# The first layer's attention of a two-layer encoder, issued in a written order

## The chip, the cores and the metric

The kernel runs on one core of one Trainium2 chip. The metric is the device time of one execution in microseconds (us), as the median of several runs. All arithmetic is on 32-bit floating point data. A profile of one execution shows every instruction of the engines: PE (TensorE, matmuls), DVE (VectorE), ACT (ScalarE), POOL (GpSimd), and SP (SyncE, which issues most transfers).

## The reference

An input of 256 tokens with 1024 features goes through two residual layers. Layer 0 has two mixers side by side on one input projection; layer 1 has another kind of attention; each layer ends with an MLP of 4096 hidden features with squared ReLU. The change concerns layer 0:

```python
hn = rms_norm(h, norm_mix_g[layer])
proj = hn @ ab_w_in[j]                                   # 1024 x 2304
qa, ka, va, qb, kb, vb = jnp.split(proj, split_ab, axis=-1)
# mixer A: 8 query heads, 2 key/value heads of 64, norm per head, rotary
qa = apply_rope(rms_norm(qa.reshape(b, s, 8, 64), a_q_norm_g[j]), cos_ax, sin_ax)
ka = apply_rope(rms_norm(ka.reshape(b, s, 2, 64), a_k_norm_g[j]), cos_ax, sin_ax)
o_a = gqa_attention(qa, ka, va)
# mixer B: 8 heads of 64, a bias by distance on the logits
o_b = dilated_attention(qb, kb, vb, rel_bias)
h = h + jnp.concatenate([o_a, o_b], axis=-1) @ ab_w_out[j]
```

## The kernel before, in words

**Weights.** All weights lie in HBM as chunks of 128 x 2048 numbers (1 MB), in the order of their use. SP loads a chunk into one of three `raw` buffers. `split_piece` splits it in pieces: ACT casts a piece to a rounded high part (`whi`, line 222), DVE subtracts to get the low part (`wlo`, line 223); each piece is 512 columns in the first five chunks and 1024 after them. There is room for the halves of four chunks. When the last piece of a chunk is split, SP is told to load the chunk three places on. A product is then three matmuls, high x high, high x low and low x high (`mm3`, lines 264 to 266). How far the splitting runs ahead is set by counters: each quarter chunk that PE uses calls `quarter`, which calls `pump`, which splits pieces up to `LEAD` = 4 quarters ahead.

**Layer 0.** Up to line 956 the order is written by hand: the projections of q, k and v of mixer A, their sums of squares, the rotation (`rope_a`), and the norms. `norms` runs on POOL: it adds the sums, raises them to the power -1/2 (line 325) and improves the result by one Newton step of four operations (lines 326 to 329), first for the 4 key norms, then for 18 numbers (16 query norms and the 2 of the row); three scalings follow. `scale_k` multiplies the rotated keys by their norms on DVE, `turn_k` transposes them on PE and copies them four times on ACT (`kdA`, each of two heads in its own half of the partitions and in the other half). Between these stand the steps of `qk_b(0)`, a generator: 4 + 4 steps of 12 matmuls for q and k of the first half of mixer B's heads, then the turn of q and the copies of k (`kdB` twice on ACT, `klB` on DVE).

**The attention** (`attention`) goes over 16 heads, 8 of A and 8 of B. A head has: scores on PE (line 850, 851), row maxima on DVE, exponentials with sums on ACT, a normalisation on DVE, four transposes on PE (line 407), a copy of these on ACT (`pts`), and for two heads together the products with the values on PE (line 396), copied as high part on ACT and low part on DVE to `OT`. Between the heads a filler feeds PE: the second half of mixer B's q and k, its values (`v_b`), and the first half of the output projection (`out_first`); `SHARE_AB` says how many of its steps go to each head. Here the program's order is only the input of a planner, which gives each engine an order of its own by costs and priorities, so that an engine may be ahead of the program's order. The second half of the output projection (`out_second`) and the MLP follow, also planned. PSUM has four banks for projections, two for scores, and two that transposes and value products share.

Of the kernel before, what the change touches and what calls it, by code (L numbers as in the profile page):

```python
# [111 lines left out]
SHARE_AB = (0, 2, 1, 0, 0, 1, 2, 2)  # L112
# [54 lines left out]
def encoder(ctx: ExitStack, tc: tile.TileContext, x, xg, wall, grow, const, onehot, relb, out):  # L167
# [34 lines left out]
    at = {"take": 0, "piece": 0, "quarter": 0}  # L202
# [9 lines left out]
    def split_piece(cast=nc.scalar.copy):  # L212

        i, q = divmod(at["piece"], 4)
        n = 2 if i >= 5 else 1
        at["piece"] += n
        if q % 2 == 0:
            parts[i, q // 2] = [wp.tile([P, CW // 2], F32R, name=z, tag=z, bufs=W_BUFS) for z in ("whi", "wlo")]
        hi, lo = parts[i, q // 2]
        raw = raws[i][:, 512 * q:512 * (q + n)]  # L220
# [16 lines left out]
    def quarter(n=2):  # L237

        at["quarter"] += 1
        pump(n)  # L240
# [68 lines left out]
    mhalf = cp.tile([P, 18], F32, name="mhalf")  # L309
# [45 lines left out]
    def attention(heads, fill, dst):  # L355
# [8 lines left out]
        def maxima(h):  # L364
            if h < n:
                prob[h] = sp.tile([P, NT, S], F32, name="prob", tag="prob", bufs=3)
                sums[h] = small(2)
                heads[h]["max"](h, sb[h], prob[h])
# [5 lines left out]
        def norm(h):  # L374
            if h < n:
                r = small(2)
# [50 lines left out]

    def scaled_softmax(scale, nscale):

        nb = {}  # L430

        def mx(h, sb, p):
            m, nb[h] = small(2), small(2)
# [47 lines left out]
    def out_first(name, src, acc):  # L481
        for c in range(2):
            i, w = take(name, c, 4)
# [163 lines left out]
    with tc.tile_pool(name="l0", bufs=1) as lp:  # L647
# [57 lines left out]
        sums = sp.tile([P, NT, 10], F32, name="sums", tag="sums", bufs=1)  # L705
        st = sp.tile([P, NT, 9], F32, name="st", tag="st", bufs=1)
        fa = lp.tile([P, NT, 9], F32, name="fa")
        kr = sp.tile([P, NT, P], F32, name="kr", tag="pts", bufs=3)
        part, rk = small(4), small(4)
        ua = cp.tile([P, NT], F32, name="ua")  # L710
        eu = small(2)
        qr = {}

        def rs0(t):
            return fa[:, t, 8:9]
# [10 lines left out]
        def sums_q(t):  # L726
            sq = work()
            nc.scalar.activation(sq, acc[t], AF.Square)
            nc.vector.reduce_sum(sums[:, t, 0:8], sq.rearrange("p (h e) -> p h e", e=64), axis=AX.X)

        def sums_k():
            sk = work()
            for t in range(NT):
                nc.scalar.activation(sk[:, cols(t)], acckv[t][:, :P], AF.Square)
            for t in range(NT):
                nc.vector.reduce_sum(sums[:, t, 8:10], sk[:, cols(t)].rearrange("p (h e) -> p h e", e=64), axis=AX.X)

        def norms():
            mean_of(part, ua)
            nc.gpsimd.tensor_scalar(eu, ua, EPS, None, op0=OP.mult)  # L740
            for t in range(NT):
                nc.gpsimd.tensor_scalar(sums[:, t], sums[:, t], 1.0 / 64, eu[:, t:t + 1], op0=OP.mult, op1=OP.add)
# [5 lines left out]
            f = fa.rearrange("p t h -> p h t")[:, 0:8]  # L748
            nc.gpsimd.tensor_scalar(fq, f, 0.125, None, op0=OP.mult)
            nc.gpsimd.tensor_scalar(nfq, f, -0.125, None, op0=OP.mult)  # L750
# [11 lines left out]
        def scale_k():  # L762
            for t in range(NT):
                for gq in range(2):
                    nc.vector.tensor_scalar(kr[:, t, cols(gq, 64)], kr[:, t, cols(gq, 64)],
                                            rk[:, 2 * t + gq:2 * t + gq + 1], None, op0=OP.mult)

        def turn_k():
# [14 lines left out]

        def spread():
            rsp = o_bank()
            row_scales(rsp, 0, rs0)
            nc.scalar.copy(rs_b, rsp[:, :S])

        def qk_b(half):
            i, w = take("qkB", 2 * half, 8)  # L790
# [10 lines left out]
            i, w = take("qkB", 2 * half + 1, 8)  # L801
            kb = mm_bank()
            for m in range(2):
                for z in range(2):
# [4 lines left out]
                    if (m, z) == (1, 1 - half):  # L809
                        for t in range(NT):  # L810
                            nc.scalar.activation(q[:, cols(t, S)], pb[:, cols(t, S)], AF.Copy, scale=rq0[:, t:t + 1])
                    quarter()
                    yield
            pt = mm_bank()
            for m in range(2):
                for t in range(NT):
                    nc.tensor.transpose(pt[:, m * S + t * P:m * S + t * P + P],
                                        q[:, t * S + m * P:t * S + m * P + P], flip)
            two = slice(2 * half, 2 * half + 2)
            stack(qB, halves(pt), (two, ALL))  # L820
            kf = work()
            nc.vector.tensor_tensor(halves(kf), halves(kb), rs_b[:, None, :].to_broadcast([P, 2, S]), op=OP.mult)
            for s in range(2):
                own, other = cols(s, 64), cols(1 - s, 64)
                hs = slice(4 * half + s, 4 * half + s + 3, 2)
                nc.scalar.copy(kdB[own, hs], halves(kf[own]))
                nc.vector.tensor_tensor(klB[own, hs], halves(kf[own]), kdB[own, hs].bitcast(F32), op=OP.subtract)
                nc.scalar.copy(kdB[other, hs], halves(kf[own]))
            yield

        def v_b():
            va = [mm_bank() for _ in range(NT)]
            for j in range(2):
                i, w = take("vB", j, 4)
# [25 lines left out]
        def head_b(h):  # L860
# [3 lines left out]
            def mx(n, sb, p):  # L864
                m, nb[0] = small(2), small(2)
# [4 lines left out]
                nc.vector.tensor_scalar(nb[0], m, -1.0, None, op0=OP.mult)  # L870
# [3 lines left out]
            def ex(n, sb, p, l):  # L874
                for i in range(NT):
                    nc.scalar.activation(p[:, i], p[:, i], AF.Exp, bias=nb[0][:, i:i + 1],
# [10 lines left out]
        with tc.manual_schedule():  # L887
# [62 lines left out]
            split(1)  # L950
            next(b0)
            turn_q(0)
            next(b0)
            split(1)
            for t in range(NT):
                rope_a(kr[:, t], acckv[t][:, :P], 2, 2, t)
            split(1)
            turn_q(1)
            next(b0)
            scale_k()  # L960
            for n in range(4):
                next(b0)
                if n < 2:
                    split(2)
            values_a()
            turn_k()
            next(b0)
            spread()
        for j in range(2):
            load_bias(j)  # L970

        oacc = {}
        def filler():
            b1 = qk_b(1)
            for _ in range(2):
                next(b1)
                yield
            yield from b0
            yield from b1
            yield from v_b()  # L980
            yield "second"
            yield from out_first("outA", OT, oacc)

        fl = filler()
        phase = [0]

        def fill(h, part):
            if phase[0] == 0:
                n = 1 if h < 7 else 100
            else:  # L990
                n = SHARE_AB[h - 8] if part == 0 and h < 16 else 0
            if h < 0:
                n = 1
            for _ in range(n):
                r = next(fl, None)
                if r == "second":
                    phase[0] = 1
                    return
                if r is None and n == 100:
                    return  # L1000

        attention([head_a(h) for h in range(HA)] + [head_b(h) for h in range(HB)], fill, OT)
        for _ in fl:
            pass
# [5 lines left out]
    with tc.tile_pool(name="l1", bufs=1) as lp:  # L1010
# [44 lines left out]
        def latent():  # L1055
# [6 lines left out]
            uu, eu, f = small(6), small(2), small(6)  # L1062
# [141 lines left out]
```

## Time and profile before

| what | value |
|---|---|
| median of 3 runs | 577.69 us (576.15 to 577.76) |
| the profiled execution | 576.51 us |
| its span, first to last instruction | 574.5 us |
| granted TensorE clock, mean over the span | 0.993 |
| PE busy, share of the span | 559.0 us, 97% |
| DVE busy | 397.8 us, 69% |
| ACT busy | 329.6 us, 57% |
| POOL busy | 39.6 us, 7% |

The span is what the profile's times count in; the execution takes 2.0 us more than its span. A line of the profile names the source line, the engine, the operation, what it writes and reads, and its shape. Ends of matmuls are modelled and overlap their followers, so that a busy PE is not yet a PE at its pace.

### The profile page before, as it was taken

The numbers are of one execution on the slowest core, as the hardware profiler recorded it, in microseconds if no ns is written. First come the engines' busy times: TensorE is split into PE (matmuls) and PEld (weight loads), VectorE is DVE, ScalarE is ACT, GpSimd is POOL, SyncE is SP. The second block draws the span as 40 slices with busy tenths as digits, with TensorE's granted clock in tenths as the row PEclk, the third lists the DMA queues.
The fourth block names the chain that finished last, engine by engine and source line by source line (L and its number), as shares of the span: only waits on it lengthen the run. The fifth ranks groups of instructions, "written<-read, shape, count | busy, mean of one in ns | idle before, by whom it ended". The sixth has DMA issues, their size and how long they took to land.

```text
span 574.5 us, 8124 instructions
## 1 busy us (share of the span) xinstructions
PE 559.0 (97%) x3044; PEld 463.0 (81%) x3044; DVE 397.8 (69%) x715; ACT 329.6 (57%) x609; POOL 39.6 (7%) x67
## 2 busy tenths in 40 slices
PE   8969999999999999999999999999999999999994
PEld 4869777788888888888889877678888888888884
DVE  4987998487666756666688888668566656756645
ACT  5858997465455454545556597756445454544513
POOL 3590000000000000000002100000000000000002
PEclk9998999999999999999999999999999999999998
DMA  8883263345455564555526223244545454554201
GB/s 282 352 283 139 74 227 127 143 163 204 174 193 184 184 219 152 214 176 191 185 108 221 74 97 124 74 163 167 201 165 211 166 209 163 204 203 164 74 1 73
DMA packets 16087, 96.64 MB, mean 168 GB/s; under 512 B 1794, under 2 KB 3074, under 8 KB 5296
## 3 DMA queue, kind: packets, MB, share of 16 engines
q1 hardware_dynamic: 15040, 94.38, 45.4%
q10 hardware_dynamic: 720, 1.07, 0.5%
q0 software_dynamic: 288, 0.68, 0.5%
q8 instruction: 24, 0.39, 0.3%
q14 instruction: 15, 0.12, 0.1%
HBM read 95.05 MB, written 1.06 MB: 167 GB/s over the span
## 4 chain that ended last, share of the span: by engine, by line
PE 83%; DVE 4%; ACT 3%; DMA 3%; POOL 3%; issue 2%; SPq 0%; POOLq 0%; DVEq 0%; ACTq 0%
PE s L537 19%; PE mm L265 14%; PE mm L264 14%; PE mm L266 14%; PE s L538 10%; PE o L396 3%; PE s L1161 2%; PE o L407 2%; DMA xh<-in_x 2%; DVE wlo L223 1%; DMA raw<-in_wall 1%; POOL sm L325 1%; PE o L457 1%; POOL sm L326 1%; ACT prob L439 1%
## 5 line engine op out<-in xcount | busy, mean ns | idle before, releaser
L223 DVE TENSOR_TENSOR wlo<-raw,whi 128x1024 fp32r<-128x1024 f32 (+1 forms) x182 | 208.7, 1164 | 99.4 <-ACT whi L222 99.0
L222 ACT CAST whi<-raw 128x1024 fp32r<-128x1024 f32 (+1 forms) x181 | 178.1, 1005 | 92.5 <-PE mm L266 46.4
L537 PE MATMUL s<-hTs,whi 128*128 128x512 f32 x480 | 168.6, 393 | 0.2
L538 PE MATMUL s<-hTs,wlo 128*128 128x256 f32 x480 | 134.5, 280 | 0.0
L537 PEld LDWEIGHTS s<-hTs,whi 128*128 128x128 f32 x480 | 90.1, 188 | 21.1 <-DVE hTs L465 1.1
L264 PE MATMUL mm<-whi,h2h 128*128 128x512 f32 x252 | 99.6, 396 | 0.0
L265 PE MATMUL mm<-wlo,h2h 128*128 128x512 f32 x252 | 99.5, 395 | 0.0
L266 PE MATMUL mm<-whi,h2l 128*128 128x512 f32 x252 | 99.0, 396 | 0.0
L538 PEld LDWEIGHTS s<-hTs,wlo 128*128 128x128 f32 x480 | 90.4, 188 | 1.4
L530 ACT CAST h2h<-work 128x256 fp32r<-128x256 f32 x64 | 25.5, 402 | 56.8 <-DVE work L529 56.8
L264 PEld LDWEIGHTS mm<-whi,h2h 128*128 128x128 f32 x252 | 47.3, 188 | 11.9 <-ACT h2h L530 0.9
L266 PEld LDWEIGHTS mm<-whi,h2l 128*128 128x128 f32 x252 | 47.2, 187 | 11.5 <-DVE h2l L531 0.3
L265 PEld LDWEIGHTS mm<-wlo,h2h 128*128 128x128 f32 x252 | 47.4, 188 | 9.8
L527 ACT COPY work<-s 128x256 f32<-128x256 f32 x60 | 22.1, 368 | 46.9 <-PE s L538 46.9
L528 DVE TENSOR_TENSOR work<-s,work 128x256 f32<-128x256 f32 x60 | 25.3, 422 | 17.3 <-ACT work L527 17.3
L531 DVE TENSOR_TENSOR h2l<-work,h2h 128x256 fp32r<-128x256 f32 x64 | 26.9, 423 | 14.6 <-ACT h2h L530 14.6
L529 DVE SCALAR_TENSOR_TENSOR work<-work 128x256 f32<-128x256 f32 x64 | 27.0, 425 | 2.1
L264 PE MATMUL mm<-whi,hTs 128*128 128x256 f32 (+1 forms) x80 | 27.8, 348 | 0.6 <-ACT hTs L904 0.6
L266 PE MATMUL mm<-whi,hTs 128*128 128x256 f32 (+1 forms) x80 | 27.2, 340 | 0.0
L265 PE MATMUL mm<-wlo,hTs 128*128 128x256 f32 (+1 forms) x80 | 27.1, 338 | 0.0
L265 PE MATMUL mm<-wlo,OT 128*128 128x512 f32 x64 | 26.3, 411 | 0.0
L264 PE MATMUL mm<-whi,OT 128*128 128x512 f32 x64 | 26.1, 408 | 0.0
(230 smaller groups left out, 775.2 us busy)
## 6 DMA issues: line engine op xcount, KB each, us to landing
raw<-in_wall SPq DMA_DIRECT2D x84, 1024.0 KB, 4.8
bias<-line_d SPq DMA_DIRECT2D x4, 384.0 KB, 4.2
raw<-in_wall SPq DMA_DIRECT2D x4, 256.0 KB, 5.6
raw<-in_wall SPq DMA_DIRECT2D x2, 512.0 KB, 7.4
xh<-in_x SPq DMA_DIRECT2D x1, 1024.0 KB, 11.6
xgt<-in_xg SPq DMA_DIRECT2D x2, 256.0 KB, 7.9
kc<-in_const SPq DMA_DIRECT2D x1, 512.0 KB, 8.8
grw<-in_grow POOLq DMA_DIRECT2D x1, 512.0 KB, 3.9
```

Of the source, the lines that this page charges most:

```text
L222: cast = cast(hi[:, s], raw)
L223: nc.vector.tensor_tensor(lo[:, s], raw, hi[:, s].bitcast(F32), op=OP.subtract)
L264: nc.tensor.matmul(out, ah, bh, start=first, stop=False)
L265: nc.tensor.matmul(out, ah, bl, start=False, stop=False)
L266: return nc.tensor.matmul(out, al, bh, start=False, stop=last)
L527: nc.scalar.copy(v[:, 0], bank[:, S:])
L528: nc.vector.tensor_tensor(v[:, 0], bank[:, :S], v[:, 0], op=OP.add)
L529: nc.vector.scalar_tensor_tensor(v[:, 1], v[:, 0], 0.0, v[:, 0], op0=OP.max, op1=OP.mult)
L530: nc.scalar.copy(hi, v[:, 1])
L531: nc.vector.tensor_tensor(lo, v[:, 1], hi.bitcast(F32), op=OP.subtract)
L537: nc.tensor.matmul(bank, wh, hTs[:, k].rearrange("p a t -> p (a t)"), start=k == 0, stop=False)
L538: nc.tensor.matmul(bank[:, S:], wl, hT[0][:, k], start=False, stop=k == 7)
```

## The change

Three things change in layer 0.

1. After the norms, nothing is planned any more: a string, `ORDER_AB`, says letter by letter which step comes next, and every engine takes its instructions in that order. The letters are: `c` cast of a piece on ACT, `l` its subtraction on DVE (with the load that it frees); `q`, `r` the turns of A's queries; `p`, `x`, `k` rotation, scaling and turn of A's keys; `n`, `m` norms and their scalings; `d`, `s` the spread of the row norm over partitions; `u` A's values; `i` the first bias loads; `a`, `b` the next step of `qk_b(0)` and `qk_b(1)`, `v` of B's values, `o` of the output projection's first half; and for the next head or pair `S` scores, `M` maxima, `E` exponentials, `N` normalisation, `T` transposes, `P` copy of these, `V` value products, `K` copies of their result. `pump` is off meanwhile.
2. POOL keeps the sums and the two powers. The Newton step becomes three operations on DVE (`newton`), for the keys and for the 18 others, the scalings of the norms and of the keys go to ACT.
3. Of A's keys, the copies in the other half read the first copies. Of B's keys, the copies in the other half are no longer made by ACT but by transfers from one half of the partitions to the other, issued from POOL's queue.

Small tiles of two numbers get 12 buffers instead of 4. The core of the diff:

```diff
-SHARE_AB = (0, 2, 1, 0, 0, 1, 2, 2)
+ORDER_AB = (
+    "clqcalclccrlclpcaacaxaanadlklaiSumaMsESbclbMESabSNTMablEcNNPbMSTcbPaTPElMlVb"
+    "KSNbEMcTPNvaETSlbcVMKNbPSvTENlcPMvbvlESTPMNvclbvVETSvNKMclbTPPScSMENvVETPMEN"
+    "SKvoMTPSNoVKcETSPMoElSNMNVTlcPKooTloEPMNETPNocVTPlKVKo")
...
-        cast = cast(hi[:, s], raw)
-        nc.vector.tensor_tensor(lo[:, s], raw, hi[:, s].bitcast(F32), op=OP.subtract)
-        if q + n == 4:
-            load(i + RAW_BUFS)
+    def split_piece(cast=nc.scalar.copy):
+        cast = cast_piece(cast)
+        low_piece()
         return cast
...
         at["quarter"] += 1
-        pump(n)
+        if not at["hand"]:
+            pump(n)
...
         def norms():
-            rsqrt(sums[:, :, 8:10], 4, rk)
-            nc.gpsimd.tensor_copy(st[:, :, 0:8], sums[:, :, 0:8])
-            nc.gpsimd.tensor_copy(st[:, :, 8], ua)
-            rsqrt(st, 18, fa.rearrange("p t h -> p (t h)"))
-            nc.gpsimd.tensor_scalar(rq0, fa[:, :, 8], 0.125, None, op0=OP.mult)
-            nc.gpsimd.tensor_scalar(fq, f, 0.125, None, op0=OP.mult)
-            nc.gpsimd.tensor_scalar(nfq, f, -0.125, None, op0=OP.mult)
+            for n in (slice(0, 2), slice(2, 11)):
+                nc.gpsimd.tensor_tensor(fa[:, :, n], sums[:, :, n], mhalf...[:, :, n], op=OP.pow)
+        def newton(n):
+            u, y = sums[:, :, n], fa[:, :, n]
+            nc.vector.scalar_tensor_tensor(u, u, -0.5, y, op0=OP.mult, op1=OP.mult)
+            nc.vector.tensor_tensor(u, u, y, op=OP.mult)
+            nc.vector.scalar_tensor_tensor(y, u, 1.5, y, op0=OP.add, op1=OP.mult)
+        def norms_end():
+            newton(slice(2, 11))
+        def scales():
+            nc.scalar.activation(rq0, fa[:, :, 10], AF.Copy, scale=0.125)
+            nc.scalar.activation(fq, f, AF.Copy, scale=0.125)
+            nc.scalar.activation(nfq, f, AF.Copy, scale=-0.125)
         def scale_k():
+            newton(slice(0, 2))
             for t in range(NT):
                 for gq in range(2):
-                    nc.vector.tensor_scalar(kr[...], kr[...], rk[...], None, op0=OP.mult)
+                    nc.scalar.activation(kr[...], kr[...], AF.Copy, scale=fa[:, t, gq:gq + 1])
...
                 nc.scalar.copy(kdA[own, s], pk[own, :S])
-                nc.scalar.copy(kdA[other, s], pk[own, :S])
+            for s in range(2):
+                nc.scalar.copy(kdA[other, s], kdA[own, s].bitcast(F32))
...
                 nc.scalar.copy(kdB[own, hs], halves(kf[own]))
+            yield
+            for own, other, hs in sides:
                 nc.vector.tensor_tensor(klB[own, hs], halves(kf[own]), kdB[own, hs].bitcast(F32), op=OP.subtract)
-                nc.scalar.copy(kdB[other, hs], halves(kf[own]))
+                nc.gpsimd.dma_start(kdB[other, hs], kdB[own, hs])
...
-        attention([head_a(h) for h in range(HA)] + [head_b(h) for h in range(HB)], fill, OT)
+            steps = {"a": b0, "b": qk_b(1), "v": v_b(), "o": out_first("outA", OT, oacc),
+                     **attention_steps([head_a(h) for h in range(HA)] + [head_b(h) for h in range(HB)], OT)}
+            for c in "".join(ORDER_AB).replace(" ", ""):
+                next(steps[c]) if c in steps else once[c]()
+        at["hand"] = False
```

`attention_steps` holds the same instructions as `attention`, each step of a head as a function of its own. In `qk_b` the scaling of q, the turn of q, the split of q, the copies of k and their low parts with the transfers are now steps of their own at the end.

## Rows read from the trace of the kernel before

**Rows 1.** Busy time by stretch: PE, PEld, DVE, ACT, POOL; granted clock; DMA.

```profile
38.60:43.30 4.70, 0.03 (x1) 0.00 (x0) 2.39 (x3) 1.24 (x4) 3.82 (x7) 1.00 0.74 258
43.30:47.10 3.80, 3.77 (x19) 3.77 (x20) 1.33 (x4) 3.46 (x6) 0.00 (x0) 0.55 0.57 233
47.10:106.00 58.90, 58.58 (x379) 46.62 (x379) 49.99 (x137) 49.89 (x118) 0.00 (x0) 1.00 0.39 139
106.00:118.60 12.60, 12.60 (x61) 9.99 (x60) 8.74 (x11) 6.58 (x13) 0.00 (x0) 1.00 0.38 129
118.60:125.00 6.40, 6.28 (x38) 5.18 (x36) 6.05 (x8) 4.47 (x8) 1.08 (x2) 1.00 0.31 100
125.00:300.00 175.00, 175.00 (x879) 146.66 (x880) 113.84 (x164) 86.44 (x132) 0.00 (x0) 1.00 0.51 186
```

**Rows 2.** Timeline of PE: first and last of the stage, the gap, the slow stretch.

```profile
27.40 0.60 PE L759 MATMUL o<-kc,qr 128*128 128x128 f32 x4
...
43.33 0.39 PE L850 MATMUL s<-kdA,qA 128*128 128x256 f32 x1 [4.71 <-ACT kdA L775]
...
43.85 0.42 PE L266 MATMUL mm<-whi,hTs 128*128 128x256 f32 x1
...
47.06 0.32 PE L265 MATMUL mm<-wlo,hTs 128*128 128x256 f32 x1
...
118.40 0.39 PE L266 MATMUL mm<-whi,OT 128*128 128x512 f32 x1
```

**Rows 3.** Timeline of POOL, where the norms are, and later in layer 1.

```profile
30.77 0.66 POOL L326 TENSOR_TENSOR sm<-sm 128x4 f32<-128x4 f32 x1
...
33.01 3.23 POOL L325 TENSOR_TENSOR sm<-st,mhalf 128x18 f32<-128x18 f32 x1
36.32 4.75 POOL L326 TENSOR_TENSOR sm<-sm 128x18 f32<-128x18 f32 x1
...
317.13 0.21 POOL L326 TENSOR_TENSOR sm<-sm 128x6 f32<-128x6 f32 x1
```

**Rows 4.** Timeline of DVE, beside the norms.

```profile
33.59 0.69 DVE L223 TENSOR_TENSOR wlo<-raw,whi 128x512 fp32r<-128x512 f32 x1
...
36.37 4.63 DVE L223 TENSOR_TENSOR wlo<-raw,whi 128x1024 fp32r<-128x1024 f32 x4
```

**Rows 5.** Timeline of PE: distances from start to start, kind by kind.

```profile
35.06 0.28 PE L264 MATMUL mm<-hTs,whi 128*128 128x256 f32 x1
...
36.00 0.28 PE L266 MATMUL mm<-hTs,wlo 128*128 128x256 f32 x1
...
60.38 1.08 PE L396 MATMUL o<-pts,vA 128*64 128x256 f32 x8
...
63.10 0.60 PE L407 MATMUL o<-kc,prob 128*128 128x128 f32 x4
63.45 0.37 PE L265 MATMUL mm<-hTs,whi 128*128 128x256 f32 x1
...
112.33 0.40 PE L265 MATMUL mm<-wlo,OT 128*128 128x512 f32 x1
...
113.73 0.39 PE L265 MATMUL mm<-wlo,OT 128*128 128x512 f32 x1
```

**Rows 6.** Timeline of ACT: one copy of mixer A keys.

```profile
42.55 0.35 ACT L774 CAST kdA<-o 64x256 fp32r<-64x256 f32 x1
```

**Rows 7.** The casts of the weights (line L222) from 20 to 106 us.

```profile
L222 ACT CAST whi<-raw x27: 604/1048/1096, 20.3 to 101.3; 128x1024 fp32r<-128x1024 f32 x19, 128x512 fp32r<-128x512 f32 x8
```

**Rows 8.** Groups of ACT instructions from 47 to 107 us: busy us, mean ns.

```profile
L410 ACT COPY pts<-o 128x512 f32<-128x512 f32 x16 | 9.4, 585 | 0.7 <-PE o L407 0.4
...
L876 ACT ACTIVATE prob<-prob,sm 128x256 f32<-128x256 f32 x16 | 8.0, 504 | 0.7 <-DVE sm L377 0.7
```

**Rows 9.** DMA issues from POOL's queue: KB, us to landing.

```profile
grw<-in_grow POOLq DMA_DIRECT2D x1, 512.0 KB, 3.9
oh<-in_onehot POOLq DMA_DIRECT2D x1, 66.0 KB, 6.6
```

More of the change, by code (lines that the diff above doesn't have):

```diff
@@ L201, in encoder @@
     raws, parts, done = {}, {}, set()
-    at = {"take": 0, "piece": 0, "quarter": 0}
+    at = {"take": 0, "piece": 0, "quarter": 0, "low": [], "hand": True}
     def load(i, pieces=1):
@@ L210, in load, with cast_piece @@
             nc.sync.dma_start(raws[i][:, s], wall[i, :, s])
-    def split_piece(cast=nc.scalar.copy):
+    def cast_piece(cast=nc.scalar.copy):
         i, q = divmod(at["piece"], 4)
@@ L426, in attention, with attention_steps, scores, maxima @@
         values(n // 2 - 1)
+    def attention_steps(heads, dst):
+        n = len(heads)
+        sb, prob, sums, pts, banks, out = {}, {}, {}, {}, {}, {}
+        def scores(h):
+            sb[h] = s_bank()
+            heads[h]["scores"](sb[h])
+        def maxima(h):
+            prob[h] = sp.tile([P, NT, S], F32, name="prob", tag="prob", bufs=3)
+            sums[h] = small(2, 12)
+            heads[h]["max"](h, sb[h], prob[h])
+        def exps(h):
+            heads[h]["exp"](h, sb.pop(h), prob[h], sums[h])
+        def norm(h):
+            r = small(2, 12)
+            nc.vector.reciprocal(r, sums[h])
+            for i in range(NT):
+                nc.vector.tensor_scalar(prob[h][:, i], prob[h][:, i], r[:, i:i + 1], None, op0=OP.mult)
+        def turned(h):
+            flipped = heads[h]["flip"]
+            banks[h] = t_bank()
+            for c in range(NT):
+                for i in range(NT):
+                    q = NT - 1 - i if flipped else i
+                    nc.tensor.transpose(banks[h][:, c * S + q * P:c * S + q * P + P], prob[h][:, i, cols(c)],
+                                        flip if flipped else ident)
+        def kept(h):
+            pts[h] = sp.tile([P, 512], F32, name="pts", tag="pts", bufs=3)
+            nc.scalar.copy(pts[h], banks.pop(h))
+        def values(j):
+            out[j] = o_bank()
+            for c in range(NT):
+                for s in range(2):
+                    nc.tensor.matmul(out[j][64 * s:64 * s + 64, :S], heads[2 * j + s]["v"](c),
+                                     pts[2 * j + s][:, cols(c, S)], start=c == 0, stop=c == NT - 1)
+        def split_values(j):
+            ob = out.pop(j)
+            nc.scalar.copy(dst[0][:, j], ob[:, :S])
+            nc.vector.tensor_tensor(dst[1][:, j], ob[:, :S], dst[0][:, j].bitcast(F32), op=OP.subtract)
+        return {c: map(f, range(k)) for c, f, k in (
+            ("S", scores, n), ("M", maxima, n), ("E", exps, n), ("N", norm, n), ("T", turned, n), ("P", kept, n),
+            ("V", values, n // 2), ("K", split_values, n // 2))}
     def scaled_softmax(scale, nscale):
@@ L482, in out_first @@
         for c in range(2):
-            i, w = take(name, c, 4)
+            i, w = take(name, c, 4, not at["hand"])
             acc[c] = [mm_bank() for _ in range(NT)]
@@ L774, in turn_k @@
                 nc.scalar.copy(kdA[own, s], pk[own, :S])
-                nc.scalar.copy(kdA[other, s], pk[own, :S])
+            for s in range(2):
+                own, other = cols(s, 64), cols(1 - s, 64)
+                nc.scalar.copy(kdA[other, s], kdA[own, s].bitcast(F32))
             for s in range(2):
@@ L782, in values_a, with spread_d @@
                 nc.scalar.activation(vA[:, t], acckv[t][:, P:2 * P], AF.Copy, scale=rs0(t))
+        dgs = []
+        def spread_d():
+            for t in range(NT):
+                dgs.append(sp.tile([P, P], F32, name="dg", tag="dg", bufs=4))
+                nc.vector.tensor_scalar(dgs[t], ident, rs0(t), None, op0=OP.mult)
         def spread():
             rsp = o_bank()
-            row_scales(rsp, 0, rs0)
+            for t in range(NT):
+                nc.tensor.matmul(rsp[:, cols(t)], ones, dgs[t], start=True, stop=True)
             nc.scalar.copy(rs_b, rsp[:, :S])
         def qk_b(half):
-            i, w = take("qkB", 2 * half, 8)
+            i, w = take("qkB", 2 * half, 8, False)
             pb = mm_bank()
@@ L800, in qk_b @@
                     yield
-            i, w = take("qkB", 2 * half + 1, 8)
+            i, w = take("qkB", 2 * half + 1, 8, False)
             kb = mm_bank()
@@ L808, in qk_b @@
                         done.add(i)
-                    if (m, z) == (1, 1 - half):
-                        for t in range(NT):
-                            nc.scalar.activation(q[:, cols(t, S)], pb[:, cols(t, S)], AF.Copy, scale=rq0[:, t:t + 1])
                     quarter()
                     yield
+            for t in range(NT):
+                nc.scalar.activation(q[:, cols(t, S)], pb[:, cols(t, S)], AF.Copy, scale=rq0[:, t:t + 1])
+            yield
+            kf = work()
+            nc.vector.tensor_tensor(halves(kf), halves(kb), rs_b[:, None, :].to_broadcast([P, 2, S]), op=OP.mult)
             pt = mm_bank()
@@ L818, in qk_b @@
                                         q[:, t * S + m * P:t * S + m * P + P], flip)
+            yield
             two = slice(2 * half, 2 * half + 2)
             stack(qB, halves(pt), (two, ALL))
[L821 to L825, printed above, removed]
+            yield
+            sides = [(cols(s, 64), cols(1 - s, 64), slice(4 * half + s, 4 * half + s + 3, 2)) for s in range(2)]
+            for own, other, hs in sides:
                 nc.scalar.copy(kdB[own, hs], halves(kf[own]))
+            yield
+            for own, other, hs in sides:
                 nc.vector.tensor_tensor(klB[own, hs], halves(kf[own]), kdB[own, hs].bitcast(F32), op=OP.subtract)
-                nc.scalar.copy(kdB[other, hs], halves(kf[own]))
+                nc.gpsimd.dma_start(kdB[other, hs], kdB[own, hs])
             yield
@@ L949, in encoder @@
             norms()
[L950 to L1000, printed above, removed]
@@ L1002, in encoder @@
[L1002 to L1004 removed]
+            oacc = {}
+            steps = {"a": b0, "b": qk_b(1), "v": v_b(), "o": out_first("outA", OT, oacc),
+                     **attention_steps([head_a(h) for h in range(HA)] + [head_b(h) for h in range(HB)], OT)}
+            once = {"c": cast_piece, "l": low_piece, "d": spread_d, "s": spread, "n": norms_end, "m": scales,
+                    "q": lambda: turn_q(0), "r": lambda: turn_q(1), "k": turn_k, "u": values_a, "x": scale_k,
+                    "p": lambda: [rope_a(kr[:, t], acckv[t][:, :P], 2, 2, t) for t in range(NT)],
+                    "i": lambda: [load_bias(j) for j in range(2)]}
@@ L1006, in encoder @@
+            for c in "".join(ORDER_AB).replace(" ", ""):
+                next(steps[c]) if c in steps else once[c]()
+            assert all(next(z, "end") == "end" for z in steps.values()) and not at["low"]
+        at["hand"] = False
     out_second("outA", OT, oacc, G_MLP)
```

55 lines of the change are left out of this document (30 added, 25 removed).

## The prediction, made before the change was run

> **What bounds the kernel now.** I read the busy time by stretch first. PE is busy in almost all of the span, and after the first layer's attention it does not stop (175.00 of 175.00 us between 125 and 300) [rows 1], so whatever the attention gives up shifts the rest to the left one for one. Inside the stage there is one hole, 38.6 to 43.3, in which PE does nothing, and behind it a stretch at a granted clock of 0.55 [rows 1]. The timeline of PE names the releaser: the first score matmul waits 4.71 us for the copied keys [rows 2], and the keys wait for the norms. The timeline of POOL shows why these are late: the 18-wide power takes 3.23 us, and then a multiply of 18 numbers takes 4.75, where one of 6 takes 0.21 elsewhere [rows 3]. DVE runs four subtractions of weights back to back in those very microseconds [rows 4]: POOL stands until DVE lets go. Elsewhere in the stage PE shows as busy, so its loss has to be found by distances from start to start.
>
> I count PE's work from 27.40 (the first turn of q) to the end of the first output projection, 118.40 + 0.23 = 118.63 [rows 2], by the loops of the code and the distances of [rows 5]: 192 matmuls of 256 columns for q and k of mixer B and 64 for scores at 0.94/8 = 0.1175 are 30.1 us; 144 of 512 columns (values of B, output projection) at 1.40/6 = 0.2333 are 33.6; 24 groups of four transposes or spreads at 0.35, plus 0.09 for the change of kind (0.37 busy for 0.28), are 10.6; the turn of k 0.25; 8 value products at 1.05 (the 1.08 overlaps its follower) are 8.4. Sum 82.9. The stretch is 91.23 long, so PE lost 8.3 us: 4.7 in the hole, 1.45 at the low clock (15 matmuls in 47.06 - 43.85 = 3.21 us instead of 1.76), and 2.2 in small waits of a few tenths.
>
> **The change part by part.**
>
> *Norms.* Four Newton operations, two copies and three scalings leave POOL; the two powers stay. The first power ends at 30.7, and the 18-wide one can start at 30.77, where the first multiply stood, instead of 33.01, and ends at 30.77 + 3.23 = 34.0 [rows 3]. DVE takes six small operations (0.1 to 0.2 us each, 0.7 in all; DVE has no row for them in this form, so I bound them by 0.3 and 1.5; the upper end is worth 0.8). By the written order DVE stands before them with the same pieces that it finished at 36.37 [rows 4], so the norms are ready at about 36.7, not 42.0, and the power has 2.7 us to spare. A hold of POOL by the two 512-wide subtractions that DVE has there (0.69 each [rows 4]) costs nothing.
>
> *First score.* After the norms: four scalings of k, now on ACT and narrower than the copy of [rows 6], some 0.26 each; the turn of k, 0.4; four copies of keys at 0.35 [rows 6], of which two now read the first two; handoffs of 0.05 to 0.1. With the norms of k at 36.4 that is 36.4 + 1.1 + 0.7 (PE is in a step of B) + 0.4 + 1.4 = 40.0 to 40.1. PE has until 27.40 + 12.4 = 39.8 the 96 matmuls of the first half of B (11.3 us) and three turns (1.1), written ahead of the first score. So the hole shrinks from 4.7 to 0.3 us, and the low clock behind it goes.
>
> *Order.* I then walked the string: every engine takes its instructions as written, each starts when the engine is free, its inputs have landed and its buffer is released. From the first score to the ninth (first head of B) PE meets no wait, so S8 starts at 40.1 + 26.7 = 66.8 (8 scores 3.8, spread 0.4, 8 steps of b 11.3, 6 turns of probabilities 2.6, 2 value products 2.1, 2 turns of B 0.9, 4 steps of v 5.6). Behind that I find new waits, all on ACT or the buffers. (1) At the first step of o, 78.9: its second bank of four in rotation is that of v, which ACT empties only after P8, a cast, E9, E10, P9, E11 and K3, that is 0.5 + 1.0 + 1.0 + 1.0, a wait for T9, then 0.5 + 1.0 + 0.3 and 0.7 for the copy, durations by [rows 7, 8] (an E is two of 0.50, copies scale with their width): PE waits 1.6. (2) At the last value product: turns and value products rotate through two banks, and its bank is that of V6, free once P15, then K6's copy and K6's subtraction are done; T15 covers 0.4, PE waits 1.6. In the kernel before the output projection's second half fills such places; a written region ends before it. (3) T9, V5 and the rest: 0.7. With the 0.3 these are 4.2 us. So the region ends at 27.40 + 70.4 + 4.2 = 102.0 and the output projection (48 x 0.2333, three turns: 12.5) at 114.5 instead of 118.63: 4.1 us gained. Whether PE's clock falls for a wait of 1.6 us no row shows; after the 4.71 it did. The bounds are 0 and 1.45 for each of the two; I take 0, for the clock is 1.00 in every other stretch of [rows 1].
>
> *Second key copies.* ACT loses four copies of B's keys at 0.6 (2.5 us) and POOL issues four transfers. The first half's keys are copied at 53.2 and needed at 66.8; the second half's at 70.7, issued by 71.4, and needed at S12, 78.5. Rows of POOL's queue land in 3.9 and 6.6 us [rows 9]: 75.3 to 78.0, so nothing is lost, with 0.5 us to spare at the slower one.
>
> *Weights.* The string holds 20 casts, 5 narrow and 15 wide. The kernel before had done 19 wide ones at the same point of PE's work (106.1) [rows 7], because its order lets ACT run ahead. Four wide pieces, 4 x 1.16 = 4.6 us of DVE (4.63 for four [rows 4]), move behind the region, where DVE is busy 8.74 of 12.60 and 6.05 of 6.40 [rows 1]. Only two of the seven pieces in that stage are needed before 114.5 and five before 123, and DVE idles 3.9 us there, so most is hidden. Between 0 and 4.6 I take 0.5, near the lower end since the free time is there.
>
> Sum: 8.3 - 4.2 - 0.5 = 3.6 us gained. The profiled execution took 576.51, and would take 572.9; the median of the runs is 577.69, 1.18 above it, and I predict for the median 574.1. About 0.3%, 1.7 us, is what a measurement can tell from no change.
>
> **The rivals.** *New waits don't appear* (o's bank is free earlier, the last value product finds its bank): 3.2 more, 577.69 - 6.8 = 570.9. For it speaks that these two waits each hang on a row of handoffs that may be shorter; against it, that the buffers are as few as before. Chance 0.13.
>
> *Hand-offs cost more than I took.* A fixed order has no planner's slack: at five places PE waits behind some six hand-offs each; 0.1 us more at each is 5 x 0.6 = 3.0: 577.1. The 2.2 us of small waits before speak for it. Chance 0.16.
>
> *The norms still come late.* If POOL's power held DVE as DVE held POOL's multiply, DVE's subtractions would stand for 3.2 us, Newton would end at 39.9 and the first score at 43.3: 574.1 + 3.2 = 577.3, or 578.8 if the low clock returns. The rows speak against it: DVE's subtraction at 33.59 took 0.69 in the middle of POOL's power [rows 3, 4]. Chance 0.06. The Trainium skill (SBUF — State Buffer, SBUF: two separate sides) calls the shared pair of ports an exclusive lock that whoever starts first keeps for a whole instruction. By that rule the time would be 577.3, by the rows 574.1; the trace agrees for POOL behind DVE (4.75 for 0.21), and differs for DVE behind POOL (0.69 as ever).
>
> *Slower: the transfers are held.* POOL must write their descriptors, and POOL can be held: if both transfers of the second half were held like the multiply, 2 x 4.75 + 6.6 = 16.1 from 70.7 is 86.8, S12 would be 8.3 late; 1.3 of it hides in o's wait: +7.0, 581.1. It decides from a landing of about 12.5 us on. Against it: DVE's longest run there is one wide subtraction (1.2 us) and a few short ones, not four. Chance 0.05. The same section of the Trainium skill warns that a transfer issued from POOL starves for descriptors while DVE has the pair; no row here shows such a transfer.
>
> *Split debt.* If the four pieces stand ahead of the turns for the MLP in DVE's queue, PE waits up to 4.6 there: 574.1 + 4.1 = 578.2. Against it speaks DVE's 3.9 us of free time. Chance 0.06.
>
> **How the numbers follow.** The forecast holds 0.54, with its own range 572.3 to 575.9. Faster by over 0.3% (below 576.0) are the forecast, the first rival and a little of the second: 0.54 + 0.13 + 0.03 = 0.70. Within 0.3%: 0.12 of the second, 0.05 of the late norms, 0.04 of the debt: 0.21. Slower (above 579.4): the held transfers 0.05 and the worse ends of the other three 0.04: 0.09. Leaving out some 0.05 below and 0.15 above, and holding the two bounds of the clock (574.1 + 2.9 = 577.0), the range is 570.9 to 577.5.
>
> **What would show it.** The first score starts near 40 and PE's gap before it is under 1 us, with a clock of 1.00 from 38 to 48. POOL has no multiply, and its wide power ends near 34 to 35. PE waits for ACT's copy of v at the first step of o, and for a bank at the last value product, some 1.6 us each; the output projection ends near 114.5. POOL's transfers land within 7 us. The prediction is wrong if PE waits more than 5 us in all between 40 and 102, if a weight-load wait appears between 114 and 125, or if the clock falls again.

## The result and the profile after

The kernel after takes 568.03 us (567.76 to 568.15), the kernel before, run beside it, 577.13: a ratio of 0.984, with a 95% interval of 0.983 to 0.986. The change gains 9.1 us; 3.6 were forecast, and the time lies 2.9 us below the low end of the range. The span fell from 574.5 to 566.0.

Busy time by stretch of the kernel after (PE, PEld, DVE, ACT, POOL; granted clock; DMA), to be read beside [rows 1]:

```profile
25.70:38.90 13.20, 12.97 (x108) 12.57 (x107) 12.39 (x33) 10.66 (x24) 6.82 (x7) 1.00 0.48 180
38.90:47.10 8.20, 8.20 (x71) 8.18 (x70) 7.56 (x15) 7.63 (x25) 0.00 (x0) 1.00 0.59 216
47.10:98.00 50.90, 50.90 (x325) 40.62 (x323) 44.11 (x123) 42.21 (x100) 2.49 (x4) 1.00 0.45 152
98.00:110.70 12.70, 12.70 (x65) 10.03 (x65) 12.23 (x16) 9.18 (x16) 0.00 (x0) 1.00 0.67 248
125.00:300.00 175.00, 175.00 (x911) 148.53 (x910) 115.84 (x163) 88.26 (x133) 3.06 (x4) 1.00 0.51 183
```

The hole and the stretch at a clock of 0.55 are gone. The timeline of PE in the kernel after, beside [rows 2]:

```profile
20.37 1.02 PE L1019 MATMUL o<-oh,rb 33*8 33x512 f32 x2
...
25.74 0.60 PE L833 MATMUL o<-kc,qr 128*128 128x128 f32 x4
...
36.84 0.33 PE L846 MATMUL o<-kc,kr 128*128 128x128 f32 x1
37.32 0.33 PE L846 MATMUL o<-kc,kr 128*128 128x128 f32 x1
...
38.92 0.28 PE L938 MATMUL s<-kdA,qA 128*128 128x256 f32 x1
...
79.01 0.39 PE L276 MATMUL mm<-whi,OT 128*128 128x512 f32 x1
...
96.09 0.66 PE L469 MATMUL o<-kc,prob 128*128 128x128 f32 x4
96.50 0.47 PE L277 MATMUL mm<-wlo,OT 128*128 128x512 f32 x1
...
97.73 0.40 PE L276 MATMUL mm<-whi,OT 128*128 128x512 f32 x1
98.06 1.08 PE L480 MATMUL o<-pts,vB 128*64 128x256 f32 x8
...
110.74 0.39 PE L601 MATMUL s<-hTs,whi 128*128 128x512 f32 x1
```

The first score starts at 38.92 and not at 43.33. The second bank of the output projection's first step is written at 79.01 without a wait, and between the last transposes (96.09) and the last value product (98.06) stand six matmuls of the output projection. The MLP begins at 110.74 and not at 118.63: 7.9 of the 8.5 us of span are gained by then. One row of ACT's timeline in the kernel after belongs to this, the copies of mixer B's values out of their banks:

```profile
79.82 1.27 ACT L931 ACTIVATE vB<-mm,fa 128x512 f32<-128x512 f32 x2
```

The norms in the kernel after, on POOL and then on DVE, beside [rows 3, 4]:

```profile
28.89 4.62 POOL L807 TENSOR_TENSOR fa<-sums,mhalf 128x4 f32<-128x4 f32 x2
...
69.65 1.23 POOL L916 DMA_DIRECT2D kdB<-kdB  x2 [16.43 <-ACT kdB L912]
```

```profile
29.72 1.33 DVE L230 TENSOR_TENSOR wlo<-raw,whi 128x512 fp32r<-128x512 f32 x2
...
36.50 0.18 DVE L815 SCALAR_TENSOR_TENSOR fa<-sums,fa 128x18 f32<-128x18 f32 x1
```

The two powers end at 33.5, and DVE's two subtractions under them took 0.67 each; one beside an idle POOL, at 24.60, took 0.69. The transfers of mixer B's second key copies landed after 4.0 us (median of 4); the last two were issued by 70.9, and the first score that reads them starts at 77.75 without a wait.

### The profile page after: what moved, and what is told of

Its sections match the earlier page's. It is cut to its first block, busy times and chain, and to the rows that moved or that the text cites. A ratio compares the mean times of both kernels' runs of the same rounds, so it can differ in the third digit from the quotient of the medians.

```text
span 566.0 us, 8115 instructions
## 1 busy us (share of the span) xinstructions
PE 555.5 (98%) x3044; PEld 461.6 (82%) x3044; DVE 399.1 (71%) x717; ACT 328.5 (58%) x612; POOL 33.5 (6%) x58
## 3 DMA queue, kind: packets, MB, share of 16 engines
HBM read 95.05 MB, written 1.06 MB: 170 GB/s over the span
## 4 chain that ended last, share of the span: by engine, by line
PE 89%; DMA 3%; ACT 3%; DVE 2%; POOL 1%; issue 1%; SPq 0%; POOLq 0%; DVEq 0%; ACTq 0%
PE s L601 20%; PE mm L276 15%; PE mm L278 15%; PE mm L277 15%; PE s L602 10%; PE s L1205 2%; DMA xh<-in_x 2%; PE o L408 2%; PE o L480 1%; PE o L469 1%; PE o L419 1%; DMA raw<-in_wall 1%; PE o L521 1%; PE mm L601 1%; ACT whi L223 1%
```

## The experiments

Times are medians; the kernel before had 576.9 to 577.3 beside these runs. The first seven look for what makes the hole and what closes it.

**1. The norms alone** on the kernel before (`norms`, `newton`, `scale_k` as in the change; ScalarE's part behind the scaling of the keys):

```diff
             scale_k()
+            norms_end()
+            scales()
             for n in range(4):
```

> The kernel before, with the norm part of the change alone: Newton steps on VectorE, the scalings of norms and keys on ScalarE; the planner's order and all else stay. Theory A, the hole of 4.7 us ahead of the first score belongs to the late norms: with the norms at about 36 to 37 the first score starts near 39.5, the low clock behind it is gone, and the time falls by 5 to 6 us (to about 572). Theory B, it belongs to what stands ahead of the keys in the engines' queues: the low key parts still stand behind DVE's four wide subtractions of weights, which end at about 41 to 41.5, so that the second score matmul waits until about 42, and only 2 to 3 us are gained.

573.21 us, a ratio of 0.9945 (0.9933 to 0.9958): 3.6 us gained, between the two. The timeline of ACT in this kernel:

```profile
36.27 1.06 ACT L776 ACTIVATE kr<-kr,fa 128x64 f32<-128x64 f32 x4 [4.27 <-DVE fa L751]
...
37.54 3.87 ACT L222 CAST whi<-raw 128x1024 fp32r<-128x1024 f32 x4
41.44 0.63 ACT L793 ACTIVATE vA<-mm,fa 128x128 f32<-128x128 f32 x2
41.95 0.36 ACT L785 CAST kdA<-o 64x256 fp32r<-64x256 f32 x1
```

The norms are there at 36.7, and still the key copies begin at 41.95, because four casts and the values stand ahead of them in ACT's queue. PE stands 2.72 us where the trace names ACT's `vA` as releaser. In the profiled execution the low clock did not come.

**2. Values behind the keys**, one exchange in the kernel before, with the norms as late as ever:

```diff
-            values_a()
             turn_k()
+            values_a()
             next(b0)
```

> The kernel before with two lines exchanged: ACT scales the values of mixer A (which needs the norms) behind the copies of its keys and not ahead of them. POOL's norms are as late as before, near 42. Theory A (the norms): head 0's softmax can't start before 42.5, so at most 1 us is gained, and POOL's multiply still takes 4 to 5 us. Theory B (the queues): the four key copies run from 37.3 to 38.8, the first score's first matmul starts near 39, the second waits for the low key parts behind DVE's four subtractions until about 42: 2 to 3 us gained, as much as by the norms alone.

575.67 us, 0.9981 (0.9972 to 0.999): 1.2 gained. The timeline of PE:

```profile
38.38 0.28 PE L850 MATMUL s<-kdA,qA 128*128 128x256 f32 x1
42.37 0.58 PE L264 MATMUL mm<-whi,hTs 128*128 128x256 f32 x1 [3.71 <-ACT vA L782]
```

The first score comes 5 us earlier, and the hole only moves behind it: the next matmuls, a step of mixer B, wait for ACT's `vA`, which empties a bank and needs the norms. Neither theory had this bank.

**3. Norms and cleared queues.** Experiment 1, with `values_a` behind `turn_k` and two of the four wide pieces behind both:

```diff
-                if n < 2:
+                if n < 1:
                     split(2)
-            values_a()
             turn_k()
+            values_a()
+            split(2)
```

> The norm part of the change on the kernel before, and besides the queues cleared by hand: two of the four wide subtractions and the scaling of the values stand behind the keys. The order of the attention is still the planner's. Theory A: as the norms alone, 5 to 6 us gained, nothing more. Theory B: the low key parts are ready near 39.5, the first score starts near 39 with no hole and no low clock, 5 to 6 us gained where the norms alone gave 2 to 3. Either way some 3 to 4 us of the whole gain of 9.1 us are left for the written order and the transfers.

573.73 us, 0.9945 (0.9932 to 0.9957): as the norms alone, so Theory B's number failed. Two casts (1.98 us) still stood ahead of the key copies, which came at 39.5. In the profiled execution the clock fell to its half behind a gap of 1.20, which it did not in that of experiment 1: 15 matmuls from 42.54 to 45.74 took 3.20 us instead of 1.76. So the equal time does not show that the cleared queue is worth nothing here.

**4. The pieces alone**, in the kernel before:

```diff
                 next(b0)
-                if n < 2:
-                    split(2)
             values_a()
             turn_k()
+            split(4)
```

> The kernel before with one edit: the four wide pieces that stood between the steps of mixer B's first half are split behind the turn of the keys. POOL keeps the whole norms, the order of the attention stays the planner's. Theory P (POOL's multiply of 18 numbers is long only because DVE runs four subtractions without a break beside it): the multiply takes 0.2 to 0.7 us, the norms are ready near 37.5, the keys near 40, the hole is under 1.5 us and the low clock gone; 3 to 6 us gained, with up to 1 us lost by later weights. Theory Q (the multiply is long of itself, or the norms are late for another reason): still above 3 us, and under 1 us gained.

575.94 us, 0.9981 (0.9972 to 0.999). Of the four wide subtractions beside POOL's multiply two are left. POOL's and DVE's timelines:

```profile
36.67 2.49 POOL L326 TENSOR_TENSOR sm<-sm 128x18 f32<-128x18 f32 x1
```

```profile
36.72 2.35 DVE L223 TENSOR_TENSOR wlo<-raw,whi 128x1024 fp32r<-128x1024 f32 x2
```

The multiply takes 2.49 instead of 4.75. Theory P is right about what holds the multiply. Its 0.2 to 0.7 us could not come with two subtractions left, and its number for the time is wrong: the keys still stood behind `vA`, PE waited 2.42 and 0.70, and the clock fell.

**5. Both moves together**, nothing else: experiment 4 with `values_a` behind `turn_k`.

> The kernel before with the norms left on POOL, and both queues cleared by two moves of lines: the four wide pieces are split behind the turn of the keys, and the values of mixer A are scaled behind the copies of its keys. The attention's order stays the planner's. Theory (the place in the queues is what counts, where Newton is done doesn't matter): as much as with Newton on VectorE and cleared queues, 2.5 to 4 us gained. Rival (PE's filler needs the bank that the scaling of the values frees, and that needs the norms near 40): the first score is near 39, but PE then waits for the filler, and at most 2 us are gained.

572.18 us, 0.9913 (0.9899 to 0.9926): 5.1 us gained by moved lines, with Newton on POOL and the planner's order. The rival was right about where PE waits, and the wait was short:

```profile
38.29 0.28 PE L850 MATMUL s<-kdA,qA 128*128 128x256 f32 x1
39.98 0.39 PE L264 MATMUL mm<-whi,hTs 128*128 128x256 f32 x1 [1.40 <-ACT vA L782]
```

**6. The kernel after with Newton on POOL:**

```diff
-                nc.gpsimd.tensor_tensor(fa[:, :, n], sums[:, :, n], mhalf...[:, :, n], op=OP.pow)
+                nc.gpsimd.tensor_tensor(w, u, m, op=OP.pow)
+                nc.gpsimd.tensor_tensor(z, w, w, op=OP.mult)
+                nc.gpsimd.tensor_tensor(z, z, u, op=OP.mult)
+                nc.gpsimd.tensor_scalar(z, z, -0.5, 1.5, op0=OP.mult, op1=OP.add)
+                nc.gpsimd.tensor_tensor(y, w, z, op=OP.mult)
...
-            newton(slice(0, 2))
```

> The kernel after with the Newton steps and the three scalings of the norms back on POOL, all else (the written order, ACT's scaling of the keys, the transfers) as in the kernel after. Theory A: POOL's multiply of 18 numbers is held by DVE again, the first score comes near 43, 4 to 6 us of the gain are lost (572 to 574). Theory B: in the written order DVE itself waits for the norms (the spread of the row norm stands ahead of the low keys), so that DVE stands still, POOL's multiply takes 0.2 to 0.7 us, the norms are ready near 38, and only 1 to 2 us are lost (569 to 570).

568.11 us, 0.9852 (0.9838 to 0.9865): no difference from the kernel after (0.9843). POOL's and DVE's timelines:

```profile
35.04 0.22 POOL L810 TENSOR_TENSOR sm<-sm 128x18 f32<-128x18 f32 x1
...
36.80 1.17 POOL L817 TENSOR_SCALAR nfq<-fa 128x16 f32<-128x16 f32 x1
```

```profile
35.02 0.21 DVE L754 TENSOR_TENSOR work<-mm,early 128x64 f32<-128x64 f32 x1
35.15 0.21 DVE L756 TENSOR_TENSOR work<-mm,early 128x64 f32<-128x64 f32 x1
35.40 0.32 DVE L758 TENSOR_TENSOR kr<-kr,work 128x128 f32<-128x128 f32 x1
36.23 0.48 DVE L858 TENSOR_SCALAR dg<-kc,fa 128x128 f32<-128x128 f32 x2 [0.51 <-POOL fa L813]
36.63 1.22 DVE L230 TENSOR_TENSOR wlo<-raw,whi 128x1024 fp32r<-128x1024 f32 x1
```

The multiply that took 4.75 us takes 0.22 here: no subtraction of weights runs beside it, but steps of the rotation. These are short, and those beside the multiply read one of their operands (`mm`) from a bank of PSUM; which of the two lets POOL through no run separates. A scaling that comes beside one wide subtraction takes 1.17. The norms are ready at 36.2 and the first score starts at 38.24, even earlier than in the kernel after. Theory A fell altogether, and B forecast a loss that is not there.

**7. All but the written order:** experiment 3 with the transfers of mixer B's second key copies. (The second copies of mixer A's keys also stay as in the kernel before.)

> Everything of the change but the written order: the kernel before with the norm part, cleared queues and the transfers of mixer B's second key copies; the attention's order is the planner's. Theory (the written order brings most): 572.5 to 573.8, so that the order itself is worth 4.5 us or more. Rival (the transfers relieve ACT in the planned order too and more than in the written one): 571.5 or less.

573.72 us, 0.9937 (0.9923 to 0.9951): the theory's number, and what experiment 3 took without the transfers (573.73). Its timeline has the gap of 1.20 ahead of the first score like that of experiment 3, but in the profiled execution the clock stayed at 1.00.

The other four take the kernel after apart.

**8. Second key copies on ACT:**

```diff
-                nc.gpsimd.dma_start(kdB[other, hs], kdB[own, hs])
+                nc.scalar.copy(kdB[other, hs], halves(kf[own]))
```

> The kernel after, with the second copies of mixer B's keys made by ACT from the same work tile as in the kernel before, and not by transfers. Theory T (ACT was nearly full between 47 and 106, so its 2.5 us count): PE waits for probabilities and copies behind ACT, and the time is 0.8 to 2.4 us longer than that of the kernel after. Rival (hidden): ACT has some 15% of idle time in that stretch of the kernel after, and the time is the same within 0.3 us.

568.98 us, 0.9863 (0.985 to 0.9877): about 1 us slower than the kernel after, as Theory T has it. The intervals of the two ratios overlap; the traces do not leave it open, for the MLP begins 0.99 later and PE's timeline has two waits that the kernel after lacks:

```profile
61.19 0.66 PE L904 MATMUL mm<-kc,work 128*128 128x128 f32 x4 [0.63 <-ACT work L897]
...
78.25 0.72 PE L469 MATMUL o<-kc,prob 128*128 128x128 f32 x4 [0.33 <-DVE prob L461]
```

**9. The output projection's second half held behind the last value product** (an order on PE alone):

```diff
     def out_second(name, src, acc, gbase):
-        last = None
+        last = at.pop("v7", None)      # the last matmul of values()
```

> The kernel after, with the second half of the output projection bound to come behind the last value product on PE (an order alone, no wait on data). Theory F (the planner moved ten of its matmuls into the written stretch, and they fill the waits that the prediction foresaw there): without them PE waits near the last transposes and at the last value product, some 0.9 and 1.6 us, and the time is 1.6 to 2.5 us longer. Rival (there was nothing to fill): PE only takes the same matmuls in another order, and the time is the same within 0.3 us.

570.11 us, 0.9883 (0.9868 to 0.9898): 2.1 us slower than the kernel after, as Theory F has it; the MLP begins 1.6 later (112.37). In the kernel after ten matmuls of `out_second` stand inside the written stretch, four ahead of the last transposes but one and six ahead of the last value product. Without them the timeline of PE reads:

```profile
95.57 0.66 PE L469 MATMUL o<-kc,prob 128*128 128x128 f32 x4
97.28 1.08 PE L481 MATMUL o<-pts,vB 128*64 128x256 f32 x8 [1.06 <-ACT pts L474]
```

**10. The bank that the prediction assumed**, forced:

```diff
+    if c == 0 and k == 0 and t == 1 and at["hand"]:
+        (ah, al), (bh, bl) = tok(src, k, t), w(k)
+        hold(nc.tensor.matmul(acc[c][t], ah, bh, start=True, stop=False), at["vb"])   # ACT's copy of vB
```

> The kernel after, with the first matmul into the second bank of the output projection's first step made to wait for ACT's copy of mixer B's first values, as the prediction assumed it by its count of the banks. Theory: the price was right and only the bank was wrong; in the kernel after that matmul starts at 79.0 and the copy would end at 80.5, so PE waits 1.5 us and the time is 1.2 to 1.8 us longer. Rival: the wait is made up later, where PE would have waited anyway, and the time is the same within 0.4 us.

569.77 us, 0.9874 (0.9861 to 0.9888): 1.7 slower than the kernel after; the MLP begins 1.9 later (112.65). The timeline of PE:

```profile
79.03 0.40 PE L278 MATMUL mm<-whi,OT 128*128 128x512 f32 x1
80.81 0.50 PE L553 MATMUL mm<-whi,OT 128*128 128x512 f32 x1 [1.39 <-ACT vB L937]
```

**11. Both waits of 9 and 10:**

> The kernel after with both waits that the prediction foresaw put in by force: the output projection's second half bound behind the last value product, and the second bank of its first step bound to ACT's copy of mixer B's first values. Alone they cost 2.1 and 1.7 us. Theory (two waits on PE's path, apart in time): they add up, 568.0 + 3.8 = 571.8, within 0.6. Rival (the later one hides behind the shift that the earlier one brings): under 570.8.

571.93 us, 0.9908 (0.9894 to 0.9921): 3.9 above the kernel after. The two add up.

## Why the prediction was wrong

The sign was right, the gain was 5.5 us too small against this comparison's kernel before, and the time 6.1 too long. Step by step:

**The step that failed: "Behind that I find new waits".** Of the 4.2 us of new waits 3.2 were two places, and neither wait exists. For (1) the prediction said that the second bank of the first step of o "is that of v". It is not: that matmul ran at 79.01, before ACT began to empty v's banks at 79.82. Here the order in which banks are asked for did not tell which one is given. For (2) it said that "a written region ends before" the output projection's second half. It does not: the planner put ten matmuls of it in front of the last value product. The prices were about right when the waits were forced: 1.6 was forecast for each, and the times were 1.7 and 2.1 longer, 3.9 together. Of the 2.1 the wait at the last value product is 1.06, and its releaser was not the bank of V6 but ACT's copy of the transposed probabilities (`pts`). So the first rival was the true case, though its 570.9 was too long by 2.9 as well; its argument was that each wait hangs on a row of handoffs, and in truth one bank was another and one gap was filled.

**A term mis-sized: "I count PE's work from 27.40".** The 192 matmuls of mixer B's q and k were all put behind the first turn of q. In the kernel before, the first step of 12 stands ahead of that turn (`next(b0)`, then `turn_q(0)`), 1.4 us; in the kernel after the turn comes first. The two traces show it: from the matmul of L931 (L1019 in the kernel after) to the first turn the kernel before takes 6.81 us with 48 matmuls between, the kernel after 5.37 with 36. The row of the kernel before, from PE's timeline:

```profile
20.59 1.02 PE L931 MATMUL o<-oh,rb 33*8 33x512 f32 x2
```

So PE's work in the stretch before was 81.5, it lost 9.7 us and not 8.3, and the small waits were 3.6 and not 2.2. In the kernel after the stretch begins at 25.74 and holds all of the 82.9; it ends at 110.74, so 2.1 us are lost, where 4.2 were forecast (3.2 in the two waits that are not there, 1.0 in all else; of the 2.1, 0.7 stand at the turn of the keys).

The sum closes: the MLP was forecast at 114.5 and began at 110.74, 3.76 earlier, of which 1.66 is the earlier start (1.4 of it the miscount) and 2.1 the smaller loss. The split debt of 0.5 did not appear. The span gained 0.6 more behind that point, in stages that the change does not touch: from the MLP's first matmul to the end the kernel before took 455.9 us and the kernel after 455.2, and all thirteen traces lie between 455.2 and 456.0. What decides within these 0.8 us stays open. And the prediction added 1.18 for the median over the profiled execution, as the kernel before had it; the median after is only 2.03 above the span, which is no more than the profiled execution before had over its span (2.01). 3.76 + 0.5 + 0.6 + 1.18 = 6.0 of the 6.1.

**The hole.** That it closes, with the low clock behind it, was right; the first score came at 38.92 for 40.1, the norms at 36.68 for 36.7, the wide power ended at 33.5 for 34.0, S8 and S12 stand at 66.14 and 77.75 for 66.8 and 78.5. The cause was only half of it. "POOL stands until DVE lets go" is shown: the multiply takes 4.75 beside four subtractions (4.63), 2.49 beside two (2.35), 0.22 beside none. But Newton on VectorE is not needed to close the hole: with it back on POOL in the written order the time is the same (experiment 6), and in the kernel before two moved blocks of lines close most of it (experiment 5, 5.1 us). What held the keys was also ACT's queue, where the values, which need the norms, stood ahead of the key copies; that queue and the four subtractions had to be cleared together, for each alone gave 1.2 or 1.3 us (experiments 2 and 4). The bank behind the values then still costs a wait of 1.40. The norms on VectorE are another way to the same end (3.6 alone). In the written order they add nothing; in the planner's order the norms with both queues fully cleared were not run, since experiment 3 left two casts ahead of the keys.

**The transfers** were given nothing beyond ACT's free time. In the written order they are worth about 1 us (experiment 8), since without them PE waits for ACT's work on mixer B; in the planner's order no gain shows (experiments 3 and 7). They landed in 4.0 us: "transfers held" did not happen.

**The written order** is worth what is left: from experiment 5 to experiment 8, which has the written order without the transfers, 572.18 - 568.98 = 3.2 us. These two differ also in where the norms are finished and the keys scaled; that Newton's place counts for nothing is shown in the written order alone, so the 3.2 is in part argued. Against experiment 7 the kernel after is 5.7 us faster, but there the gap ahead of the first score is part of it. That the written order leaves so little lost is shown by the profile: by distances from start to start, one place between 36 and 110 loses more than 0.2 us, the turn of the keys (0.7). Experiment 6 has it closed and begins the MLP 0.7 us earlier (110.05), yet ends at the same time: its lead shrinks little by little over all that follows, which takes 456.0 us there and 455.2 in the kernel after. Why was not found.

**The other rivals.** "The norms still come late" by POOL's power holding DVE did not happen: DVE's subtractions took 0.67 under the power. The Trainium skill (SBUF — State Buffer, SBUF: two separate sides) calls the shared pair of ports an exclusive lock, held for a whole instruction, that also DVE has to wait for. The trace agrees that POOL stands behind DVE, though the multiply of 18 numbers stood through four instructions and through two (4.75, 2.49) and not through one alone; it differs for DVE, which did not stand behind this power. "Hand-offs cost more" did not happen either.

## What to carry to other kernels

Before an operation is moved to another engine because it is late, look at what runs beside it and at what stands ahead of its users in their own queues: here two moved blocks of lines gave 5.1 us, and the moved operation, once the order was right, nothing. A wait that is deduced from counted buffers, or from the end of a written stretch, has to be held against the order that really results; two such waits, priced about right and absent, were 3.2 of the 4.2 us of waits foreseen here. When work is counted from a landmark, count the instructions on either side of it in each kernel, for the change may have moved them across.

## What was not expected of the hardware

- A gap on PE does not by its length decide whether the clock falls. After 2.72 us it stayed at 1.00 (experiment 1), after 2.42 and another of 0.70 it fell (experiment 4); behind the same gap of 1.20 it fell in experiment 3 and not in experiment 7. The rows behind these gaps, from the timelines of PE in experiments 4, 3 and 7:

```profile
41.41 0.38 PE L850 MATMUL s<-kdA,qA 128*128 128x256 f32 x1 [2.42 <-ACT kdA L775]
```

```profile
40.27 0.39 PE L861 MATMUL s<-kdA,qA 128*128 128x256 f32 x1 [1.20 <-ACT kdA L786]
```

```profile
40.70 0.38 PE L861 MATMUL s<-kdA,qA 128*128 128x256 f32 x1 [1.20 <-ACT kdA L786]
```

  Busy time by stretch, experiment 3 and then experiment 7:

```profile
43.30:47.10 3.80, 3.80 (x25) 3.80 (x25) 3.77 (x7) 3.45 (x7) 0.00 (x0) 0.67 0.57 207
```

```profile
43.30:47.10 3.80, 3.62 (x32) 3.44 (x31) 3.77 (x7) 3.54 (x6) 0.00 (x0) 1.00 0.59 244
```

  The 0.67, like the 0.55 of the kernel before, is a mean over a stretch that is in part at the full clock (2.4 GHz): where the clock fell it fell to the half (1.2 GHz), in experiment 3 from 42.4 to 45.8, where it is 0.50. Each trace is one execution. Of the five executions of experiment 7 two have a mean granted clock of 0.996 and 0.998 and took 573.11 and 572.75 us, and three have 0.993 and took 573.72 to 574.10, so the same kernel probably has the fall in some executions and not in others; no trace of these three shows it.

- POOL's multiply of 18 numbers was held by a run of DVE's subtractions as a whole, by four in the kernel before and by two in experiment 4. That is not so for every operation of POOL: the multiply of 4 numbers in the kernel before [rows 3] began at 30.77, under the first of two subtractions, and was done at 31.43, while the second ran until 31.96. These two, from DVE's timeline in the kernel before:

```profile
30.67 1.29 DVE L223 TENSOR_TENSOR wlo<-raw,whi 128x512 fp32r<-128x512 f32 x2
```

  What makes the difference no run shows. Beside the steps of the rotation the multiply of 18 numbers was not held either (0.22, experiment 6).
